# Splitting each block of weights with one operation of 1024 columns per engine, up to five steps ahead of its use

## The chip, the core and the metric

The kernel runs on one core of one Trainium2 chip. The core has a matrix engine (PE, TensorE; its weight loads are listed apart as PEld), a vector engine (DVE, VectorE), a scalar engine (ACT, ScalarE), a general engine (POOL, GpSimd) and a queue engine that here only issues transfers (SP, SyncE). Each engine works through its own instructions in the order in which they stand in its queue. An instruction that must wait for another engine holds up all that stands behind it on its own engine.

The metric is the time of one execution on the device, in microseconds (us); lower is better. A profile is a record of one execution: which instruction ran when on which engine, and what ended the idle time before it.

## The reference

The reference is a trunk of two layers over 256 tokens of width 2048. Each layer normalises its input, multiplies it by one wide matrix, gives the columns to two groups of heads and multiplies their gated outputs by a second matrix. Cut to what matters:

```python
for l in range(DEPTH):                                  # 2 layers
    h = rms_norm(x, norm_g[l])
    proj = jnp.einsum('btd,dc->btc', h, w_in[l])        # 2048 -> all heads' inputs
    rw_in, g_rw, q, k_at, v_at, g_at = jnp.split(proj, col_splits, axis=-1)
    rw_in = bidir_token_shift(rw_in, shift_mu[l])
    r, k, v, xw, xa = jnp.split(rw_in, rw_splits, axis=-1)
    y_rw = rwkv7_branch(r, k, v, xw, xa, ...)           # recurrent heads, both directions
    y_at = window_attention(rope(q), rope(k_at), v_at, sink[l])   # |i-j| <= 128
    mix = jnp.concatenate([y_rw * silu(g_rw), y_at * silu(g_at)], axis=-1)
    x = x + jnp.einsum('btc,cd->btd', mix, w_out[l])
return rms_norm(x, final_g)
```

Everything is float32. All that the change touches is how the two large products get their weights.

## The kernel before

**The large products.** A weight matrix is cut into blocks of 128x1024 numbers (512 KB); there are 280 of them in the two layers. A product of float32 numbers is made of three products in a faster number format (fp32r): the activations are kept as a rounded part and a rest (`XH`, `XL`, or `MH`, `ML` ahead of the second matrix), and each block of weights is split in the same way into `hi` (ACT copies the raw block into the rounded format, L215) and `lo` (DVE subtracts `hi` from the raw block, L216). A block serves eight **steps**, and each step is three matmuls: `XH` with `hi` (L273), `XL` with `hi` (L274), `XH` with `lo` (L275). Two blocks, or 16 steps, add up one output tile `pm` of 128x256. (Eight of the 280 blocks serve the values of the attention; they have a step of another shape, L513 to L515.) `wsplit` makes the split in two halves of 512 columns: ACT, DVE, ACT, DVE, so that the first four steps need the first half alone.

**Buffers.** `raw` has three buffers (pool `wrp`), `hi` and `lo` two each (pool `wsp`). So the split of one block cannot start before the last matmul of the block two before it has read its buffer.

**The order.** The steps of all blocks stand in one list (class `Stream`). `S.run(n)` writes down the next n steps. When the present block has `PREFETCH` steps left or fewer, it first writes down the load and the split of the next block. The function `window` writes 64 steps, in 14 slots, between which it writes the pieces of the recurrent heads (`scan_p`, `scan_i`, `scan_b`) and of the attention (`scores`, `flip`, `values`). PE runs in exactly that order. For ACT, DVE and SP a scheduler sets the order when the program is built: of the instructions that it reckons ready it takes the one that was written down first, with some pieces put ahead (`scan_b` with an offset of 95). So where a split is written down, and how long it is, changes what stands before and behind it on ACT and DVE.

**Names that the prediction uses.** One window of 64 steps uses eight blocks. In it `scan_i` of one pair of heads makes two products `pg` (L718), each masked by DVE into `ge` (L724). After the second `ge`, ACT copies out `AB` (L733), a state `suv` of `scan_b` (L890), a part of `ge` (L771), the transposed `bt` (L754) and four parts `suv` (L759), which read the PSUM tile `pt`. PE then goes on with `pq` (L803). Tiles `pg`, `pn`, `pu`, `pt`, `pyt`, `pq` and `pd` take turns in two PSUM buffers (pool `ps_w`), so PE writes one of them only when the last but one has been read out. `t` (L924) is an ACT operation at the end of `scan_b`, which reads `pyt`. `duh` (L441) is an ACT operation that waits for a transfer of `dup`. In a step of the inverse inside `scan_i`, PE's `pq` (L813) waits for DVE's predicated copies `tv` and `tt` (L822, L823).

Of the kernel before, what the change touches and what calls it, by code (L numbers as in the profile page):

```python
# [50 lines left out]
    [0, 2, 5, 7, 8, 10, 12, 13],  # L51
]
PRIO_B = 95
PREFETCH = 2


def _layout():
# [71 lines left out]
def hybrid_trunk_kernel(ctx, tc, xT, wi, wv, wo, par, fing, dup, iup, sink, pos, cst, out):  # L129
# [75 lines left out]
    def wload(src):  # L205
        raw = wrp.tile([128, 1024], F32, tag="raw", name="raw")
        SY.dma_start(out=raw, in_=src)
        return raw

    def wsplit(raw):  # L210
        hi = wsp.tile([128, 1024], F32R, tag="hi", name="hi")
        lo = wsp.tile([128, 1024], F32R, tag="lo", name="lo")
        for i in range(2):
            q = slice(i * 512, (i + 1) * 512)
            A.activation(hi[:, q], raw[:, q], AF.Copy)  # L215
            V.tensor_tensor(lo[:, q], raw[:, q], hi[:, q].bitcast(F32), op=ALU.subtract)  # L216
        return hi, lo

    def halves(src, first=None):
        return [lambda: wsplit(first if first is not None else wload(src[0])), lambda: wsplit(wload(src[1]))]  # L220

    class Stream:

# [13 lines left out]
        def run(self, n):  # L237
            for _ in range(n):
                load, steps, done = self.q[0]
                if not self.ready:  # L240
                    self.ready.append(load())
                if len(self.ready) == 1 and len(steps) <= PREFETCH and len(self.q) > 1:
                    self.ready.append(self.q[1][0]())
# [15 lines left out]
    def gemm(src, operands, evac, first=None, begin=None):  # L259

        box = []

        def step(kk):
            def f(w):
                if not box:
                    box.append(ps_main.tile([128, T], F32, tag="m", name="pm"))
                    if begin:
                        begin()
                pm = box[0]
                rh, rl = operands()  # L270
                k = kk % 8
                wh, wl = w[0][:, k * 128 : (k + 1) * 128], w[1][:, k * 128 : (k + 1) * 128]
                PE.matmul(pm, wh, rh[:, kk, :], start=(kk == 0), stop=False)  # L273
                PE.matmul(pm, wh, rl[:, kk, :], start=False, stop=False)  # L274
                PE.matmul(pm, wl, rh[:, kk, :], start=False, stop=(kk == 15))  # L275

            return f

        ld = halves(src, first)
        S.add(ld[0], [step(k) for k in range(8)])  # L280
        S.add(ld[1], [step(k) for k in range(8, 16)], lambda: evac(box[0]))
# [105 lines left out]
    def queue_inputs(l):  # L387
# [136 lines left out]
        for qt in range(4):  # L524
            S.add(
                lambda qt=qt: wsplit(wload(wv[l, qt])),
                [v_step(qt * 4 + k, b) for k in range(4) for b in range(2)],
                v_evac if qt == 3 else None,
            )
# [615 lines left out]
```

## Time and profile before

| | us |
|---|---|
| median of 3 runs (1242.3 to 1247.03) | 1244.04 |
| the profiled execution, whole | 1247.3 |
| its span, first to last instruction | 1245.5 |
| busy: PE | 1184.3 (95%) |
| busy: DVE | 937.5 (75%) |
| busy: ACT | 739.9 (59%) |
| DMA queue q1, share of 16 engines | 38.5% |

The page of the profile is an overview; matmuls overlap on PE and their ends are modelled, so its 95% says that PE is seldom seen idle, not that it runs at its best. The view of the waits sums the idle time of an engine by what ended it. The timeline lists instructions with start, length, and in brackets the idle time of the engine before them and what ended it. A view by stretches of time gives busy time and the granted clock of PE in each.

The program has three kinds of stretch: the start of a layer (about 0 to 85 us and 620 to 695 us), where the products run with little beside them; the windows with recurrent heads and attention (to about 535 us, and to about 1150 us); and the second matrix's product (the rest), where PE runs steps alone.

### The profile page before, as it was taken

The page shows a single profiled execution, that of the slowest core. Times are in us where ns is not written, and L with a number is a line of the kernel's source. Part 1 is how long each engine was busy: PE and PEld are TensorE (multiplying, and loading weights), DVE is VectorE, ACT ScalarE, POOL GpSimd, SP SyncE. Part 2 cuts the span into 40 slices and gives each one's busy share as a digit, 9 for nine tenths or more (in the row PEclk, how much of TensorE's full clock was granted, in tenths as well). Part 3 has the DMA queues.
Part 4 walks back from the last instruction along what each step waited for, and adds up shares of the span by engine and source line. Part 5 has one row for each costly group of instructions (what it writes and reads, how often), then busy time and mean ns, then how long its engine had stood idle before and what let it go on. Part 6 is the DMA issues. An engine that isn't in the chain of part 4 may idle for free.

```text
span 1245.5 us, 38032 instructions
## 1 busy us (share of the span) xinstructions
PE 1184.3 (95%) x16140; PEld 1092.3 (88%) x16140; DVE 937.5 (75%) x2082; ACT 739.9 (59%) x1838; POOL 19.0 (2%) x23
## 2 busy tenths in 40 slices
PE   6989999999998999999999999999999989999996
PEld 6978888888887989989998888888888888899996
DVE  6878878887976678856666888878887766786654
ACT  6646665766565466645555656665766555675553
POOL 0000000000000000000000000000000000000000
PEclk9999999999999999999999999999999999999998
DMA  7443233322322434466554433233223324435653
GB/s 246 156 143 122 88 116 109 105 93 94 134 77 93 133 109 142 140 204 224 210 182 143 143 110 119 93 111 109 104 93 100 112 99 131 140 130 174 212 190 119
DMA packets 60410, 166.70 MB, mean 134 GB/s; under 512 B 7728, under 2 KB 22736, under 8 KB 60240
## 3 DMA queue, kind: packets, MB, share of 16 engines
q1 hardware_dynamic: 60240, 164.27, 38.5%
q8 instruction: 126, 2.06, 0.7%
q14 instruction: 44, 0.36, 0.1%
HBM read 157.43 MB, written 4.19 MB: 130 GB/s over the span
## 4 chain that ended last, share of the span: by engine, by line
PE 48%; DVE 18%; issue 16%; ACT 11%; DMA 4%; SPq 1%; POOL 0%; DVEq 0%; POOLq 0%; ACTq 0%
PE pm L273 13%; PE pm L275 11%; PE pm L274 11%; DVE lo L216 3%; DMA g<-dup 3%; PE pg L718 2%; DVE kd L665 2%; ACT hi L215 2%; DVE ge L724 2%; ACT AB L733 2%; ACT suv L759 2%; DVE lw L659 2%; ACT ge L771 1%; DMA rrot<-u 1%; ACT bt L754 1%
## 5 line engine op out<-in xcount | busy, mean ns | idle before, releaser
L273 PE MATMUL pm<-XH,hi 128*128 128x256 f32 x1664 | 498.1, 299 | 14.5 <-ACT XH L178 6.1
L275 PE MATMUL pm<-XH,lo 128*128 128x256 f32 x1664 | 471.4, 283 | 11.2 <-DVE lo L216 11.2
L274 PE MATMUL pm<-XL,hi 128*128 128x256 f32 x1664 | 470.6, 283 | 0.1
L215 ACT ACTIVATE hi<-raw 128x512 fp32r<-128x512 f32 x560 | 329.6, 625 | 212.1 <-PE pm L274 170.0
L216 DVE TENSOR_TENSOR lo<-raw,hi 128x512 fp32r<-128x512 f32 x560 | 369.0, 687 | 84.0 <-ACT hi L215 76.7
L273 PEld LDWEIGHTS pm<-XH,hi 128*128 128x128 f32 x1664 | 316.5, 190 | 40.2 <-issue 13.0
L275 PEld LDWEIGHTS pm<-XH,lo 128*128 128x128 f32 x1664 | 316.8, 190 | 14.6 <-DVE lo L216 14.4
L274 PEld LDWEIGHTS pm<-XL,hi 128*128 128x128 f32 x1664 | 317.3, 191 | 0.8 <-DVE XL L179 0.8
L273 PE MATMUL pm<-MH,hi 128*128 128x256 f32 x512 | 145.5, 284 | 2.3 <-ACT hi L215 2.3
L275 PE MATMUL pm<-MH,lo 128*128 128x256 f32 x512 | 145.2, 284 | 0.1
L274 PE MATMUL pm<-ML,hi 128*128 128x256 f32 x512 | 145.0, 283 | 0.0
L273 PEld LDWEIGHTS pm<-MH,hi 128*128 128x128 f32 x512 | 97.9, 191 | 3.2 <-ACT hi L215 2.5
L275 PEld LDWEIGHTS pm<-MH,lo 128*128 128x128 f32 x512 | 97.8, 191 | 0.4 <-DVE lo L216 0.4
L274 PEld LDWEIGHTS pm<-ML,hi 128*128 128x128 f32 x512 | 98.0, 191 | 0.0
L890 ACT ACTIVATE suv<-pu 64x128 f32<-64x128 f32 x128 | 34.5, 270 | 24.8 <-PE pcc L888 13.6
L724 DVE TENSOR_TENSOR ge<-pg,C 128x1024 f32<-128x1024 f32 x32 | 39.1, 1221 | 3.5 <-PE pg L718 3.5
L970 ACT ACTIVATE mv<-mv,mx 128x257 f32<-128x257 f32 x64 | 31.9, 504 | 15.9 <-DVE mx L967 15.9
L733 ACT ACTIVATE AB<-ge 64x512 f16<-64x512 f32 x32 | 20.2, 630 | 34.3 <-DVE ge L724 33.9
L718 PE MATMUL pg<-mv,bk 64*128 64x128 f32 x512 | 37.2, 285 | 0.0
L822 DVE CAST_PREDICATED tv<-LV,pd 128x256 f16<-128x256 uint8 x80 | 34.0, 426 | 4.1 <-PE pd L821 3.7
L815 ACT ACTIVATE QF<-pq 128x256 f16<-128x256 f32 x80 | 30.8, 385 | 6.8 <-PE pq L813 5.5
L823 DVE CAST_PREDICATED tt<-LV,pd 128x256 f16<-128x256 uint8 x80 | 34.0, 425 | 0.0
(241 smaller groups left out, 1833.7 us busy)
## 6 DMA issues: line engine op xcount, KB each, us to landing
raw<-wi SPq DMA_DIRECT2D x207, 512.0 KB, 3.8
raw<-wo SPq DMA_DIRECT2D x64, 512.0 KB, 3.8
raw<-wv SPq DMA_DIRECT2D x8, 512.0 KB, 3.6
rrot<-u SPq DMA_DIRECT2D x80, 32.0 KB, 2.3
vg<-xT SPq DMA_DIRECT2D x16, 128.0 KB, 3.6
xd<-vg SPq DMA_DIRECT2D x16, 128.0 KB, 3.6
vg<-xd SPq DMA_DIRECT2D x16, 128.0 KB, 3.5
g<-dup SPq DMA_DIRECT2D x16, 97.0 KB
```

The costliest lines, as they stand in the source:

```text
L215: A.activation(hi[:, q], raw[:, q], AF.Copy)
L216: V.tensor_tensor(lo[:, q], raw[:, q], hi[:, q].bitcast(F32), op=ALU.subtract)
L273: PE.matmul(pm, wh, rh[:, kk, :], start=(kk == 0), stop=False)
L274: PE.matmul(pm, wh, rl[:, kk, :], start=False, stop=False)
L275: PE.matmul(pm, wl, rh[:, kk, :], start=False, stop=(kk == 15))
L718: PE.matmul(pg[:, h, c * 128 : (c + 1) * 128], BK[half[h], d, c, 1 - h : 3 - h, :].rearrange("p s j -> p (s j)"), MV[half[h], d, c].rearra ...
L724: V.tensor_tensor(GEd(d), pg.rearrange("p h (c x) -> p h c x", c=NC), gm[d].unsqueeze(1).unsqueeze(1).to_broadcast([128, 2, NC, 128]), op= ...
L733: A.activation(flat(AB[half[h]]), GE[h][half[h]].rearrange("p d c s j -> p (d c) s j")[:, :, 0, :], AF.Copy)
L822: V.copy_predicated(t_sub(TC), t_mask, flat4(pd[:, :, 0:128]))
L823: V.copy_predicated(v_sub(TT), v_mask, flat4(pd[:, 0, 128:384].rearrange("p (d x) -> p d x", d=2)))
L890: A.activation(here(h), pu[half[h], :, 0:64], AF.Copy)
L970: A.activation(Sc[:, h, q, 0:257], Sc[:, h, q, 0:257], AF.Exp, scale=0.125, bias=mx[:, q : q + 1], accum_out=den[:, q : q + 1])
```

## The change

`PREFETCH` goes from 2 to 5, so the split of the next block (and its load) is written down when five steps of the present block are left. `wsplit` makes `hi` of all 1024 columns with one ACT operation and `lo` with one DVE operation. Only the very first block, which is loaded in two halves, keeps the two halves.

```diff
-PREFETCH = 2
+PREFETCH = 5
...
-    def wsplit(raw):
+    def wsplit(raw, parts=1):
         hi = wsp.tile([128, 1024], F32R, tag="hi", name="hi")
         lo = wsp.tile([128, 1024], F32R, tag="lo", name="lo")
-        for i in range(2):
-            q = slice(i * 512, (i + 1) * 512)
+        for i in range(parts):
+            q = slice(i * 1024 // parts, (i + 1) * 1024 // parts)
             A.activation(hi[:, q], raw[:, q], AF.Copy)
             V.tensor_tensor(lo[:, q], raw[:, q], hi[:, q].bitcast(F32), op=ALU.subtract)
         return hi, lo
 
     def halves(src, first=None):
-        return [lambda: wsplit(first if first is not None else wload(src[0])), lambda: wsplit(wload(src[1]))]
+        return [lambda: wsplit(first, 2) if first is not None else wsplit(wload(src[0])), lambda: wsplit(wload(src[1]))]
```

The order of PE's instructions is the same in both programs. That of POOL is the same. On SP one load of a block in each layer moves ahead of one group of four `rrot` transfers (L494) in the attention part; all other transfers stand in the same order. ACT and DVE change in many places. Three of them follow.

The first place is ACT's queue in a window with all parts of the recurrent heads, from `AB` (L733) on. Before:

```order
L733 ACTIVATE AB<-ge 64x512 x2
L890 ACTIVATE suv<-pu 64x2x64 x2
L771 ACTIVATE ge<-mv 64x6x64
L215 ACTIVATE hi<-raw 128x512
L754 ACTIVATE bt<-pt 128x768
L759 ACTIVATE suv<-pt 64x4x64 x4
L771 ACTIVATE ge<-mv 64x6x64
```

The same place in the changed kernel:

```order
L733 ACTIVATE AB<-ge 64x512 x2
L890 ACTIVATE suv<-pu 64x2x64 x2
L771 ACTIVATE ge<-mv 64x6x64
L215 ACTIVATE hi<-raw 128x1024
L754 ACTIVATE bt<-pt 128x768
L759 ACTIVATE suv<-pt 64x4x64 x3
L924 ACTIVATE t_3615<-pyt,PR 128x256
L759 ACTIVATE suv<-pt 64x4x64
```

The split ahead of `bt` is now the whole block, and `t` (L924) has moved from behind the last `suv` to ahead of it. This order with L924 stands in 12 of the 16 windows that have a `pt`.

The second place is DVE's queue ahead of the two `ge` (L724) of the same kind of window. Before:

```order
L410 TENSOR_TENSOR g<-pm,rb 128x256
L216 TENSOR_TENSOR lo<-raw,hi 128x512 x2
L412 SCALAR_TENSOR_TENSOR vg<-g 128x256
L784 COPY tv<-EYE 128x512
L724 TENSOR_TENSOR ge<-pg,C 128x2x512
```

In the changed kernel:

```order
L410 TENSOR_TENSOR g<-pm,rb 128x256
L216 TENSOR_TENSOR lo<-raw,hi 128x1024
L412 SCALAR_TENSOR_TENSOR vg<-g 128x256
L784 COPY tv<-EYE 128x512
L724 TENSOR_TENSOR ge<-pg,C 128x2x512
```

Nothing has moved here; one operation stands where two stood, and it can start only when the whole `hi` is there.

The third place is DVE's queue in the attention, behind the softmax of one head pair (L971, L973). Before:

```order
L973 TENSOR_SCALAR mv<-mv,den 128x256 x2
L897 TENSOR_TENSOR suv<-pcc,pc 64x2x64 x2
L216 TENSOR_TENSOR lo<-raw,hi 128x512 x5
L897 TENSOR_TENSOR suv<-pcc,pc 64x2x64 x2
```

In the changed kernel:

```order
L973 TENSOR_SCALAR mv<-mv,den 128x256
L897 TENSOR_TENSOR suv<-pcc,pc 64x2x64 x2
L973 TENSOR_SCALAR mv<-mv,den 128x256
L216 TENSOR_TENSOR lo<-raw,hi 128x1024 x2
L897 TENSOR_TENSOR suv<-pcc,pc 64x2x64 x2
```

The whole `lo` of the next block stands behind the same work as its first half did before.

## The prediction, made before the changed kernel was run

> **What bounds the kernel now.** I read the page's busy times first, then a table of stretches, then the waits, then the timeline at the places where the orders differ.
>
> ```profile
> PE 1184.3 (95%) x16140; PEld 1092.3 (88%) x16140; DVE 937.5 (75%) x2082; ACT 739.9 (59%) x1838; POOL 19.0 (2%) x23
> 564.00:622.00 58.00, 58.00 (x491) 58.00 (x490) 37.45 (x70) 30.74 (x62) 0.00 (x0) 1.00 0.62 218
> 70.40:83.50 13.10, 9.86 (x75) 9.17 (x76) 13.10 (x26) 8.23 (x19) 0.00 (x0) 1.00 0.35 118
> ```
>
> The columns of the last two rows are the stretch, its length, then busy time of PE, PEld, DVE, ACT, POOL, PE's clock and DMA. In the second matrix's product (564 to 622 us) PE is never idle: 58.00 of 58.00, at full clock. A better split gives nothing there. At the start of a layer (70 to 83 us) DVE is busy 13.10 of 13.10 us and PE is not. The waits say how much PE loses to splits in all:
>
> ```profile
> ACT hi L215 <- PE pm L274: 170.0, 138, 3.5
> PE pm L275 <- DVE lo L216: 11.2, 15, 1.6
> PE pm L273 <- ACT hi L215: 6.2, 4, 2.3
> PE pq L803 <- ACT suv L759: 11.6, 12, 1.5
> PEld L813 <- DVE tt L823: 4.2, 10, 0.5
> ```
>
> (Total, times, longest.) PE waits 11.2 + 6.2 = 17.4 us for splits: the most that earlier splits can give directly. ACT, for its part, waits 170 us, in 138 cases, for PE to release a `hi` buffer. So the splits already stand at the first moment at which their buffer is free; to write them down three steps sooner cannot start those sooner. It only changes their rank against other work. The fourth row is the wait that decides the rest: in 12 windows PE waits for the last `suv`.
>
> **The change part by part.** First the price of one long operation. The trace has operations of 1024 columns on both engines (`mv`, L1042 and L1043):
>
> ```profile
> L215 ACT ACTIVATE hi<-raw 128x512 fp32r<-128x512 f32 x560 | 329.6, 625 | 212.1 <-PE pm L274 170.0 <-issue 30.5 <-PE pva L515 2.6
> L216 DVE TENSOR_TENSOR lo<-raw,hi 128x512 fp32r<-128x512 f32 x560 | 369.0, 687 | 84.0 <-ACT hi L215 76.7
> L1042 ACT ACTIVATE mv<-X 128x1024 f32<-128x1024 f32 x3 | 3.0, 1048 | 0.0
> L1043 DVE TENSOR_TENSOR mv<-mv 128x1024 f32<-128x1024 f32 x3 | 3.7, 1222 | 0.0
> 209.67 1.15 ACT L215 ACTIVATE hi<-raw 128x512 fp32r<-128x512 f32 x2 [2.73 <-PE pm L274]
> ```
>
> A half takes 625 ns on ACT and 687 on DVE, a whole 1048 and 1222. But two halves back to back take 1.15 us on ACT (last row), and 1.28 or 1.29 on DVE (below), since they overlap. So a pair saves 0.10 us of ACT and 0.07 of DVE, over 279 blocks 28 and 20 us of engine time, and none of it is PE's. Against that the first half of `hi` was there after 0.63 us, the whole is after 1.05; `lo` follows 0.42 later than its first half could.
>
> [...]
>
> *Windows with all parts (10).* ACT's queue from `AB` on, in one of them, and PE's wait:
>
> ```profile
> 173.00 1.28 ACT L733 ACTIVATE AB<-ge 64x512 f16<-64x512 f32 x2 [2.10 <-DVE ge L724]
> 174.31 0.56 ACT L890 ACTIVATE suv<-pu 64x128 f32<-64x128 f32 x2
> 174.89 0.53 ACT L771 ACTIVATE ge<-mv 64x384 f32<-64x384 f32 x1
> 175.32 0.62 ACT L215 ACTIVATE hi<-raw 128x512 fp32r<-128x512 f32 x1
> 175.97 0.81 ACT L754 ACTIVATE bt<-pt 128x768 f32<-128x768 f32 x1
> 176.79 1.55 ACT L759 ACTIVATE suv<-pt 64x256 f32<-64x256 f32 x4
> 178.91 0.57 ACT L924 ACTIVATE t<-pyt,PR 128x256 f32<-128x256 f32 x1
> 178.39 0.33 PE L803 MATMUL pq<-tv,AB 64*64 64x32 f16 x11 [0.86 <-ACT suv L759]
> ```
>
> From 173.00 to 178.34 ACT has no pause, and PE starts `pq` 0.05 us after the last `suv`, having waited 0.86. Whatever is put into this queue ahead of the last `suv` is added to PE's wait. The changed order puts in two things: the whole `hi` for a half, 1.05 - 0.62 = 0.43 us, and `t` (L924), which takes 0.57 us and so pushes the next one by about 0.47 (its neighbours overlap by 0.1). Nothing covers them: **+0.90 per window**.
>
> The second place is `ge`:
>
> ```profile
> 210.33 1.29 DVE L216 TENSOR_TENSOR lo<-raw,hi 128x512 fp32r<-128x512 f32 x2
> 211.54 0.42 DVE L412 SCALAR_TENSOR_TENSOR vg<-g 128x256 f32<-128x256 f32 x1
> 212.08 1.22 DVE L724 TENSOR_TENSOR ge<-pg,C 128x1024 f32<-128x1024 f32 x1
> 213.40 1.16 PE L718 MATMUL pg<-mv,bk 64*128 64x128 f32 x16
> 214.60 1.23 DVE L724 TENSOR_TENSOR ge<-pg,C 128x1024 f32<-128x1024 f32 x1 [0.22 <-PE pg L718]
> ```
>
> `hi` starts at 209.67, when PE releases its buffer, and the first half of `lo` at 210.33. A whole `hi` ends at 210.72, `lo` runs from 210.78 to 212.00, 0.38 later than 211.62; the first `ge` ends at 213.68 instead of 213.30. The second `pg` uses its PSUM buffer and cannot start at 213.40, but at 213.74: **+0.35**. Bounds are 0 (if PE arrives later for another reason) and 0.43. In return a late PE no longer waits for `tt` ahead of L813 (4.2 us in 10 cases, 0.42 each); DVE's own queue is mostly full up to there and moves back with it, so of 0 to 0.42 I take **-0.2**. Sum 1.05 per window, bounds 0.45 to 1.3; ten windows **+10.5** (4.5 to 13).
>
> *Last two windows with a `pt` (one per layer).* They have L924 ahead too. PE waited 1.54 for `suv` there: **+0.9 each, 1.8**.
>
> *Attention.* `lo` at the third place, twice per layer:
>
> ```profile
> 446.25 1.90 DVE L216 TENSOR_TENSOR lo<-raw,hi 128x512 fp32r<-128x512 f32 x3
> 447.11 0.28 PE L275 MATMUL pm<-XH,lo 128*128 128x256 f32 x1
> 464.37 1.89 DVE L216 TENSOR_TENSOR lo<-raw,hi 128x512 fp32r<-128x512 f32 x3
> 465.11 0.39 PE L275 MATMUL pm<-XH,lo 128*128 128x256 f32 x1 [0.99 <-DVE lo L216]
> ```
>
> DVE's work ahead is the same, so the whole `lo` ends at 447.47 and 465.59, and PE starts 0.41 and 0.53 later than it did: **+1.9** for both layers (0 to 4, as the exponentials may shift).
>
> *Block behind `duh`.* At 555 ACT stands behind a transfer in both orders, and the whole block comes after it:
>
> ```profile
> 554.73 1.13 ACT L215 ACTIVATE hi<-raw 128x512 fp32r<-128x512 f32 x2
> 555.53 1.28 DVE L216 TENSOR_TENSOR lo<-raw,hi 128x512 fp32r<-128x512 f32 x2
> 556.27 0.58 PE L275 MATMUL pm<-MH,lo 128*128 128x256 f32 x1
> ```
>
> `lo` now runs 555.84 to 557.06: PE 0.8 late, but at half clock (below), so worth 0.4 to 0.8: **+0.6**.
>
> *Starts of layers.* Here lie most of the 17.4 us, and DVE has no pause. It gains 0.07 per block, five blocks 0.35; the second halves come earlier, the first parts later, and what PE no longer waits for in the middle of a block it waits for at its head. I take **0**; the bounds are -3 (0.35 saved at each of four starts, and twice that where a wait at the head of a block goes with it) and +2 (0.42 lost at the head of one block in each). The loads stand in the same order on SP but for one per layer; a late `rrot` costs at most the 1 to 2 us until a raw buffer is free, in a stretch where PE has other steps: 0.
>
> Sum: 10.5 + 1.8 + 1.9 + 0.6 + 0 = +14.8. The profiled execution took 1247.3 (its span 1245.5), 3.3 over the median of 1244.04. So 1262 on its scale, and **1259** on the median's. The bounds together give +5 to +20: 1249 to 1264.
>
> **The rivals.** *Half clock in every window (slower still).* After two long waits close together PE ran at half clock:
>
> ```profile
> 394.80:398.10 3.30, 1.76 (x48) 1.60 (x44) 1.27 (x3) 3.20 (x7) 0.00 (x0) 1.00 0.02 5
> 398.20:401.50 3.30, 3.30 (x37) 2.96 (x35) 3.14 (x8) 2.42 (x7) 0.00 (x0) 0.50 0.03 10
> 176.30:179.60 3.30, 2.44 (x58) 2.28 (x58) 1.03 (x4) 3.20 (x8) 0.00 (x0) 1.00 0.05 12
> 1005.50:1008.80 3.30, 2.37 (x35) 2.18 (x34) 1.22 (x4) 3.10 (x8) 0.00 (x0) 1.00 0.00 0
> ```
>
> With 1.76 us busy of 3.30 the next stretch had clock 0.50; with 2.37 it had not. In a window PE is busy 2.44 of 3.30 around `pq`; 0.9 less makes 1.54. So the clock may halve ten times, each for 3.4 us, which costs up to 1.7: 5 to 17 on top, 1264 to 1276. Against it: the wait must fall into one such stretch, and steps stand close on both sides. [...]
>
> *Nothing moves on balance.* If PE's later arrival frees it from DVE's waits fully (0.42 per window), the second `pg` doesn't wait, and layer starts gain their 3, what is left is 10 x 0.48 - 3 + 1 = +3 against the median of 1244: 1247. It is also the case where the change doesn't do what it says, as ACT's 170 us of waiting suggest for the five steps.
>
> *Faster.* All 17.4 us of waits for splits vanish and ACT's queue ahead of `suv` costs nothing: 1227. For it only the waits themselves; against it the full DVE in 70.40:83.50 and ACT's unbroken 173.00 to 178.34.
>
> **How the numbers follow.** Forecast 1249 to 1264: 0.65. Half clock: 0.15. Nothing on balance: 0.14. Faster: 0.06. The range reaches from 1247 into the half-clock case, 1274. A measurement of this kernel can tell about 0.5% (6.2 us) from no change: same is 1237.8 to 1250.3, the case of nothing plus the lowest corner of the forecast, 0.16; slower 0.78, faster 0.06.
>
> **What would show it.** Right: PE's wait for `suv` (L759) at L803 rises from 0.86 to about 1.75 in ten windows, 11.6 to some 22 in sum; the distance between the same `ge` of two neighbouring windows grows by about 1; the stretch of the second matrix's product stays as long as it is; ACT's busy time at L215 falls from 329.6 to about 292 (279 x 1.048) and DVE's at L216 from 369.0 to 341 (279 x 1.222). Wrong: if that wait stays at 0.86, or if it rises and a like amount goes from L813 and L275; if the first `ge` ends as early as before; if the starts of layers lose more than 3 us of waits.

## The result, and the profile after

The changed kernel took 1265.12 us (median of 4 runs, 1262.83 to 1265.89), the kernel before 1245.53 beside it (4 runs): ratio 1.0155, interval 1.0134 to 1.0176. The forecast was 1259 in a range of 1247 to 1274, and its likeliest case, slower by a wait in each window, is what happened, though 1 us above that case's own range (1249 to 1264). Most of its terms have other sizes than I gave them.

First the page of the changed kernel: busy time of each engine, then the two groups of the split (busy time, mean ns of one, idle time before it and what ended it).

```profile
span 1263.8 us, 37504 instructions
PE 1187.7 (94%) x16140; PEld 1093.9 (87%) x16140; DVE 923.2 (73%) x1803; ACT 714.3 (57%) x1559; POOL 19.3 (2%) x23
...
L216 DVE TENSOR_TENSOR lo<-raw,hi 128x1024 fp32r<-128x1024 f32 (+1 forms) x281 | 342.4, 1219 | 130.1 <-ACT hi L215 128.4
L215 ACT ACTIVATE hi<-raw 128x1024 fp32r<-128x1024 f32 (+1 forms) x281 | 296.3, 1055 | 225.3 <-PE pm L274 186.8
```

The split itself is as cheap as it was priced: 296.3 us on ACT (forecast 292) and 342.4 on DVE (341). Both engines are less busy, and the kernel is slower. On DVE the rows of the two kernels give 369.0 - 342.4 = 26.6 us less, and none of it reached the end. Now the waits (total, times, longest):

```profile
ACT hi L215 <- PE pm L274: 186.8, 139, 4.0
DVE lo L216 <- ACT hi L215: 128.4, 172, 2.5
PE pq L803 <- ACT t L924: 15.8, 12, 2.0
PE pm L273 <- ACT hi L215: 10.0, 4, 3.5
PE pm L275 <- DVE lo L216: 9.4, 12, 1.7
PE pq L813 <- DVE tt L823: 3.9, 10, 0.6
PE pq L813 <- DVE tv L822: 3.6, 13, 0.7
PE pg L718 <- DVE ge L724: 2.8, 12, 0.2
```

Two rows of the kernel before, for PE's waits at L813:

```profile
PE pq L813 <- DVE tv L822: 1.5, 5, 0.4
PE pq L813 <- DVE tt L823: 0.9, 4, 0.3
```

ACT waits for PE to release `hi` in 139 cases against 138: five steps ahead did not start the splits sooner. The third row of the first list is the window's wait, and its releaser is new: `t` (L924) where it was `suv` (L759). Its last row did not exist before. One window, ACT and then PE:

```profile
173.45 0.53 ACT L771 ACTIVATE ge<-mv 64x384 f32<-64x384 f32 x1
173.88 1.04 ACT L215 ACTIVATE hi<-raw 128x1024 fp32r<-128x1024 f32 x1
174.95 0.81 ACT L754 ACTIVATE bt<-pt 128x768 f32<-128x768 f32 x1
175.77 1.15 ACT L759 ACTIVATE suv<-pt 64x256 f32<-64x256 f32 x3
176.83 0.55 ACT L924 ACTIVATE t<-pyt,PR 128x256 f32<-128x256 f32 x1
177.40 0.38 ACT L759 ACTIVATE suv<-pt 64x256 f32<-64x256 f32 x1
...
177.43 0.33 PE L803 MATMUL pq<-tv,AB 64*64 64x32 f16 x11 [1.34 <-ACT t L924]
...
193.38 0.30 PE L813 MATMUL pq<-tv,AB 64*64 64x32 f16 x16 [0.34 <-DVE tt L823]
...
213.12 1.16 PE L718 MATMUL pg<-mv,bk 64*128 64x128 f32 x16 [0.24 <-DVE ge L724]
```

`pq` starts at 177.43, 0.05 after `t` ends (176.83 + 0.55) and well before the last `suv` ends (177.78). So PE no longer waits for the last `suv` at all: `t` stands in its place in PE's wait, not on top of it. The wait is 1.34, against 0.86. From the start of `AB` to `pq` it is 5.87 us, against 5.39, in all twelve windows.

Where the time went is read best by stretches. The table gives the time from one block's first matmul on PE to another's (a block is 24 matmuls of L273 to L275 or their like; the core has 280, worked out from the traces, one profiled execution each). The stretches 32 to 72 and 176 to 216 hold five windows each.

| blocks | before | after | halves ahead of `bt` | halves in attention | halves at three places | half buffers, only `suv` ahead |
|---|---|---|---|---|---|---|
| start to 32 | 147.9 | 146.3 | 146.6 | 145.5 | 146.3 | 143.6 |
| 32 to 72, windows | 216.4 | 223.1 | 217.9 | 223.1 | 216.6 | 215.5 |
| 72 to 80 | 45.7 | 45.8 | 43.7 | 45.3 | 44.2 | 46.3 |
| 80 to 112, attention | 134.4 | 137.2 | 138.2 | 134.5 | 134.1 | 132.3 |
| 112 to 120, `duh` | 28.5 | 29.0 | 28.5 | 29.8 | 29.8 | 25.2 |
| 120 to 152, second matrix | 92.1 | 92.1 | 91.5 | 91.5 | 92.1 | 92.1 |
| 152 to 176, start | 113.5 | 113.6 | 112.4 | 113.5 | 113.5 | 110.5 |
| 176 to 216, windows | 215.8 | 221.8 | 218.0 | 221.6 | 216.7 | 215.1 |
| 216 to 224 | 42.2 | 44.0 | 44.8 | 44.9 | 42.7 | 42.3 |
| 224 to 248, attention | 104.1 | 106.0 | 106.1 | 104.6 | 104.6 | 102.1 |
| span | 1245.5 | 1263.8 | 1252.7 | 1259.2 | 1245.5 | 1229.8 |

Of 18.3 us the ten windows have 6.7 + 6.0 = 12.7, attention 2.8 + 1.9 = 4.7, and the second matrix nothing. In both profiled executions PE stood at half clock for about as long, 31.6 and 32.0 us in all, but not at the same places: from 72 to 80 it did so only before (3.4 us), from 216 to 224 and in the first five windows only after (3.4 us each), and behind `duh` for 6.8 us before and 3.4 after. At half clock (0.50 granted in these stretches) at most half of the time is lost, so stretches with such a difference are uncertain by up to 1.7 us.

### The profile page after: what moved, and what is told of

Its sections match the earlier page's. It is cut to its first block, busy times and chain, and to the rows that moved or that the text cites. A ratio compares the mean times of both kernels' runs of the same rounds, so it can differ in the third digit from the quotient of the medians.

```text
span 1263.8 us, 37504 instructions
## 1 busy us (share of the span) xinstructions
PE 1187.7 (94%) x16140; PEld 1093.9 (87%) x16140; DVE 923.2 (73%) x1803; ACT 714.3 (57%) x1559; POOL 19.3 (2%) x23
## 5 line engine op out<-in xcount | busy, mean ns | idle before, releaser
L273 PE MATMUL pm<-XH,hi 128*128 128x256 f32 x1664 | 499.1, 300 | 15.1 <-ACT hi L215 6.6
L275 PE MATMUL pm<-XH,lo 128*128 128x256 f32 x1664 | 473.0, 284 | 9.0 <-DVE lo L216 8.7
L216 DVE TENSOR_TENSOR lo<-raw,hi 128x1024 fp32r<-128x1024 f32 (+1 forms) x281 | 342.4, 1219 | 130.1 <-ACT hi L215 128.4
L215 ACT ACTIVATE hi<-raw 128x1024 fp32r<-128x1024 f32 (+1 forms) x281 | 296.3, 1055 | 225.3 <-PE pm L274 186.8
L273 PEld LDWEIGHTS pm<-XH,hi 128*128 128x128 f32 x1664 | 317.4, 191 | 41.3 <-issue 13.0
L275 PEld LDWEIGHTS pm<-XH,lo 128*128 128x128 f32 x1664 | 318.0, 191 | 12.9 <-DVE lo L216 12.7
L273 PE MATMUL pm<-MH,hi 128*128 128x256 f32 x512 | 144.8, 283 | 3.5 <-ACT hi L215 3.5
L275 PE MATMUL pm<-MH,lo 128*128 128x256 f32 x512 | 144.6, 283 | 0.8 <-DVE lo L216 0.8
L273 PEld LDWEIGHTS pm<-MH,hi 128*128 128x128 f32 x512 | 97.4, 190 | 4.4 <-ACT hi L215 3.7
L275 PEld LDWEIGHTS pm<-MH,lo 128*128 128x128 f32 x512 | 97.3, 190 | 1.0 <-DVE lo L216 1.0
L890 ACT ACTIVATE suv<-pu 64x128 f32<-64x128 f32 x128 | 34.2, 267 | 20.7 <-PE pq L813 10.4
L724 DVE TENSOR_TENSOR ge<-pg,C 128x1024 f32<-128x1024 f32 x32 | 39.0, 1220 | 4.4 <-PE pg L718 4.1
L733 ACT ACTIVATE AB<-ge 64x512 f16<-64x512 f32 x32 | 20.1, 629 | 38.6 <-DVE ge L724 38.2
L718 PEld LDWEIGHTS pg<-mv,bk 64*128 64x128 f32 x512 | 31.1, 187 | 6.0 <-DVE ge L724 4.4
```

Source lines behind the costliest of these rows:

```text
L718: PE.matmul(pg[:, h, c * 128 : (c + 1) * 128], BK[half[h], d, c, 1 - h : 3 - h, :].rearrange("p s j -> p (s j)"), MV[half[h], d, c].rearra ...
L724: V.tensor_tensor(GEd(d), pg.rearrange("p h (c x) -> p h c x", c=NC), gm[d].unsqueeze(1).unsqueeze(1).to_broadcast([128, 2, NC, 128]), op= ...
L733: A.activation(flat(AB[half[h]]), GE[h][half[h]].rearrange("p d c s j -> p (d c) s j")[:, :, 0, :], AF.Copy)
L890: A.activation(here(h), pu[half[h], :, 0:64], AF.Copy)
```

## The experiments

**Which half of the change costs?** Theory A: the one long operation. Rival B: the five steps, which change the rank of `lo` on DVE. Each half of the change alone:

```diff
 the changed kernel, two steps:
-PREFETCH = 5
+PREFETCH = 2
 the kernel before, five steps:
-PREFETCH = 2
+PREFETCH = 5
```

> The change's kernel with splits two steps ahead as before: the one operation alone. Theory A (the single long operation costs; the five steps change only rank): the loss of 1.0155 stays, 1.013 to 1.020 of before, 1262 to 1270 us, with PE's wait at L803 again behind the last suv or t at some 1.3 us per window. Rival B (the five steps cost, since lo goes ahead of DVE's tv and tt): the time returns to before, 1.000 to 1.004, and L813's waits for tt and tv return from 6.3 + 3.9 + 3.6 to 4.2 + 0.9 + 1.5 us.

> The kernel before with splits five steps ahead, halves kept: the five steps alone. Theory A: no change, 0.997 to 1.003, as ACT waits for PE to release hi in some 140 cases either way; L803's wait stays near 0.86 per window. Rival B: most of the loss, 1.009 to 1.016, with L813's waits for tt and tv up as in the change's kernel.

Measured: one operation with two steps 1266.59 us, ratio to before 1.0179 (1.0159 to 1.0200); halves with five steps 1244.82, 0.9992 (0.9977 to 1.0007). B falls; the five steps alone change nothing that can be measured, and ACT waits for PE's release of `hi` in 133 cases there. With the one operation alone, the waits have the change's form:

```profile
PE pq L803 <- ACT t L924: 17.3, 12, 2.0
PE pq L813 <- DVE tt L823: 3.8, 10, 0.6
PE pg L718 <- DVE ge L724: 2.9, 12, 0.2
```

**Where does it cost?** The changed kernel, with halves again at chosen blocks. For the twelve ahead of `bt`:

```diff
+    nsplit = iter(range(1000))
     def wsplit(raw, parts=1):
+        if next(nsplit) % 140 in (38, 46, 54, 62, 70, 78):
+            parts = 2
```

Ahead of the first `ge` the list is (45, 53, 61, 69, 77), in the attention `range(80, 112)`, and the fourth kernel has all three.

> The change's kernel, but the twelve blocks whose hi stands ahead of bt in ACT's queue (six per layer) are split in halves. Theory A with this place: L803's wait falls from 1.34 back to 0.86 per window, 12 x 0.48 = 5.8 us, 0.994 to 0.997 of the change's kernel (1257 to 1261). Rival C (the wait at L803 only stands in for another one just behind it): L803's wait falls but L813's rises by a like amount, under 2 us in all. The half-clock stretch at 310 us may go too, 1.5 us.

> The change's kernel, but the ten blocks whose lo stands ahead of the first ge of a window in DVE's queue are split in halves. Theory A with this place: the second pg's wait for ge (2.8 + 4.4 us on PE and its loads, 0.24 each in ten windows) goes, 2 to 3 us of the loss, 0.997 to 0.9985 of the change's kernel (1261 to 1263). Rival C: the time is taken up by L803 or L813 behind it, under 0.5 us.

> The change's kernel with halves in 32 blocks around the attention of each layer (blocks 80 to 111 of 140) and whole blocks elsewhere. Theory A (the whole lo there is late by some 0.4 to 0.7 us at the blocks for which DVE's queue is full): the 4.6 us that these stretches lost come back, 0.9955 to 0.9975 of the change's kernel, 1259 to 1261. Rival (the loss came with the other order behind the last window, not with the length): under 1 us.

> The change's kernel with halves ahead of bt, ahead of the first ge, and around the attention, and whole blocks at the 95 or so other places of a layer. Theory A (the loss sits at these three places and the whole operation is free elsewhere): 10.5 + 1.5 + 4.5 us come back, 1247 to 1250, 0.999 to 1.004 of the kernel before. Rival (the whole operation costs a little everywhere, through ACT and DVE): 1253 or more, 1.006 and up.

| halves | median us | to before (interval) | span |
|---|---|---|---|
| ahead of `bt` | 1254.53 | 1.0085 (1.0068 to 1.0102) | 1252.7 |
| ahead of the first `ge` | 1263.91 | 1.0156 (1.0139 to 1.0173) | 1261.9 |
| in the attention | 1260.25 | 1.0123 (1.0109 to 1.0137) | 1259.2 |
| at all three | 1244.98 | 0.9995 (0.9984 to 1.0007) | 1245.5 |

Ahead of `bt`, more came back than expected: 11.1 us of span, not 5.8. Its waits at L803 and L813:

```profile
PE pq L803 <- ACT suv L759: 11.5, 12, 1.6
PE pq L813 <- DVE tv L822: 3.8, 9, 0.9
PE pq L813 <- DVE tt L823: 1.4, 3, 0.6
PE pg L718 <- DVE ge L724: 2.8, 12, 0.2
PE pza L622 <- DVE tt L809: 3.3, 10, 0.6
```

The order ahead of the last `suv` is the old one, and the wait at L803 with it (11.6 before). Of the 11.1 us, 9.0 lie in the ten windows. There L803 gives back 4.9 and L813 3.4, but a wait for `tt` at L622 (last row), which the changed kernel does not have, takes 3.3 again. So rival C, that one wait stands in for another, holds for L813 and L622, but not for L803. One stretch at half clock is gone as well (up to 1.7), and the rest is in no wait that the profile lists. Halves ahead of `ge` leave PE 0.9 of its 2.8 us of waits for `ge`. In the trace the distance between the same `ge` of two neighbouring windows falls from 44.0 to 43.7 us (42.9 before the change). That is too little for the comparison of times, which shows no difference from the change (1.0156 against 1.0155). Halves in the attention give 4.6 us of span back, 4.1 of it there (134.5 and 104.6 in the table). With all three the span is that of before, though 193 of 280 blocks are still split whole. So on balance the whole operation is free at those, and the loss sits at these three places; for the place ahead of `ge` the times alone do not show it.

**Is it ACT's length alone?** `hi` in halves at the twelve blocks ahead of `bt`, `lo` whole everywhere:

```diff
             A.activation(hi[:, q], raw[:, q], AF.Copy)
-            V.tensor_tensor(lo[:, q], raw[:, q], hi[:, q].bitcast(F32), op=ALU.subtract)
+        V.tensor_tensor(lo, raw, hi.bitcast(F32), op=ALU.subtract)
```

> The change's kernel with hi alone in halves at the twelve blocks ahead of bt, lo whole. If ACT's length ahead of bt is the cause there (theory A): as with both in halves, 1254 to 1257, L803's wait behind suv at 0.9 to 1.0. If DVE's length matters as well (the whole lo holds up tt): L803's wait comes back, L813's stays at 6.3 + 3.9 us, 1258 to 1261.

1285.57 us, 1.0325 of before (1.0308 to 1.0343): neither. PE's two waits in one window, and what ACT and DVE did ahead of the second:

```profile
176.74 0.33 PE L803 MATMUL pq<-tv,AB 64*64 64x32 f16 x11 [0.83 <-ACT suv L759]
180.26 0.39 PE L275 MATMUL pm<-XH,lo 128*128 128x256 f32 x1 [1.57 <-DVE lo L216]
...
177.26 0.56 ACT L924 ACTIVATE t<-pyt,PR 128x256 f32<-128x256 f32 x1
177.73 0.62 ACT L215 ACTIVATE hi<-raw 128x512 fp32r<-128x512 f32 x1
...
178.99 1.22 DVE L216 TENSOR_TENSOR lo<-raw,hi 128x1024 fp32r<-128x1024 f32 x1
```

L803's wait is as before the change, though `lo` is whole: it was set by ACT's queue (the length of `hi`, and the place of `t`, which came back with the halves), not by DVE. But the second half of `hi` now stands behind `t` on ACT, and a whole `lo` needs both: it starts at 178.99 and PE waits 1.57 for it, and after several of these waits the clock halved (last section; the mean granted clock was 0.977, against 0.987 in the changed kernel's profiled execution). Halves paid here only where both engines had them (1254.53 against 1285.57), so that the first half went all the way to PE.

**What if nothing stands ahead of `suv`?** In the kernel before, `hi` of the twelve blocks was queued behind the last `suv` (a no-wait edge in the order, `issue_after`); then also the two copies into `ge` (L771). In the changed kernel the whole `hi` was queued so:

```diff
+            if n in (38, 46, 54, 62, 70, 78):
+                es.enter_context(tc.issue_after(suv_read[-1]))
             ...
             for h in range(2):
+                with tc.issue_after(suv_read[-1]):
                     A.activation(c3(GE[h]...), c3(MV...), AF.Copy)
```

> The kernel before (halves, two steps), with the hi of the twelve blocks ahead of bt queued on ACT behind the last suv of its step. Theory A (what stands ahead of the last suv in ACT's queue is added to PE's wait): L803's wait falls from 0.86 to some 0.3 per window, 12 x 0.55 = 6.6 us less if nothing else is late, 1239 to 1243, 0.995 to 0.998 of before. Rival (the block of weights is then late, or L813 and tt bound at once behind it): within 0.2% of before.

> The kernel before with both fillers of ACT's queue, the hi of the twelve blocks and the two copies into ge (L771 there), queued behind the last suv of their step, so that bt and suv follow AB and the other suv at once. Theory A (the queue ahead of the last suv is PE's wait, 0.53 us of ge and 0.62 of hi): L803's wait of 0.86 goes to 0 in ten windows and from 1.54 to some 0.4 in the last two, 8 to 11 us less, 1234 to 1238, 0.992 to 0.995 of before. Rival (hi or ge are then late in turn, and PE waits at L275 or L866 instead): within 0.3% of before.

> The change's kernel, its whole hi of the twelve blocks queued behind the last suv. Theory A: L803's wait falls from 1.34 to 0.85, as a ge takes the place ahead; but the block's first use is some 1 us behind the last suv, and a whole hi and a whole lo need 1.05 + 1.2 us from there, so PE waits for lo at L275 by some 1.5 us in each window instead: 1270 to 1280, 1.02 to 1.03 of before. Rival (place alone counts, not length): as with halves ahead of bt, 1252 to 1256.

`hi` alone behind `suv`: 1243.67, 0.9992 (0.9981 to 1.0003), a miss. The scheduler filled the place with the second `ge`, and L803's wait stayed 0.85. With `ge` behind too: 1247.66, 1.0013 (1.0003 to 1.0024). The wait at L803 fell from 11.6 us to 0.5 in one case, and two others stand in one window in its stead:

```profile
178.42 0.39 PE L273 MATMUL pm<-XH,hi 128*128 128x256 f32 x1 [0.49 <-ACT hi L215]
179.26 0.39 PE L275 MATMUL pm<-XH,lo 128*128 128x256 f32 x1 [0.33 <-DVE lo L216]
```

0.49 + 0.33 = 0.82 for 0.86: the rival, nearly one for one. The whole `hi` behind `suv` took 1261.55, 1.0126 (1.0109 to 1.0142), less bad than expected, and worse than its rival: L803 0.85, and PE waits 0.40 for `lo`, not 1.5, since `lo` starts on DVE at once when `hi` is done (177.82). In a window ACT has one half of `hi` to place ahead and one behind, and the kernel before does just that.

**Sooner buffers.** If PE's release of `hi` is what a split waits for, tiles of half a block free it sooner, in the same memory. First alone (halves, five steps), then with the second half of `hi` and the `ge` copies behind `suv`:

```diff
-        hi = wsp.tile([128, 1024], F32R, tag="hi", name="hi")
-        lo = wsp.tile([128, 1024], F32R, tag="lo", name="lo")
+        hi = [wsp.tile([128, 512], F32R, tag=f"hi{i}", name="hi") for i in range(2)]
+        lo = [wsp.tile([128, 512], F32R, tag=f"lo{i}", name="lo") for i in range(2)]
```

> Halves five steps ahead, and hi and lo each in two tiles of 512 columns (the same memory), so that PE releases the first half's buffer half a block (1.4 us) sooner. Theory A: PE's waits for hi and lo (6.2 + 11.2 us in the kernel before) fall by up to half, but in the windows the second half of hi now stands ahead of bt where the first stood, so L803's wait stays at 0.86: 1236 to 1243, 0.992 to 0.998 of before. Rival (DVE is full where those waits lie, so sooner buffers bring nothing): 0.998 to 1.002.

> As the half buffers, and the second half of hi of the twelve blocks and the two copies into ge queued behind the last suv. Theory A: with the first half of hi split before AB, moving the rest behind the last suv no longer makes PE wait for the block: L803's wait goes (0.86 in ten windows, some 1.2 in two) and none comes at L273 or L275 for it, 8 to 11 us less than the half buffers alone, 1226 to 1235, 0.984 to 0.992 of before. Rival (lo or tt is late in turn, as DVE is): within 0.3% of the half buffers alone.

Alone: 1246.66, 0.9991 (0.9974 to 1.0008), a miss, and the rival's number. Together: 1232.31, **0.988** (0.9862 to 0.9897), faster than both kernels. The waits, of the half buffers alone and of both:

```profile
PE pq L803 <- ACT suv L759: 11.0, 11, 1.0
PE pq L813 <- DVE tt L823: 10.4, 10, 1.1
PE pm L275 <- DVE lo L216: 5.3, 8, 2.0
```

```profile
PE pza L622 <- DVE tt L809: 7.6, 10, 0.8
PE pm L275 <- DVE lo L216: 5.7, 8, 2.0
PE pq L813 <- DVE tt L823: 3.8, 10, 1.1
```

The total came out in the expected range, though 14.4 us below the half buffers alone and not 8 to 11; the reason did not come out as expected. The wait at L803 is gone (0.5 us is left, in one case), but a wait of 0.8 for `tt` (L809) takes its place ahead of L622, and the windows are nearly as long as before (215.5 and 215.1 for five, against 216.4 and 215.8). The gain over before lies at the layer starts, 4.3 + 3.0, behind `duh`, 3.3, and in the attention, 2.1 + 2.0. Waits for splits account for a part of it: those for `lo` at L275 fell from 11.2 us to 5.7, those for `hi` at L273 from 6.2 to 5.1. The clock may account for another part, in these two executions: the one of before stood at half clock for 6.8 us behind `duh` and 3.4 at the second start, this one at neither (up to 3.4 and 1.7 us). The ratio 0.988 is not the clock, as its mean over all runs is 0.990 here and between 0.989 and 0.990 before; where the gain lies is shown in part only. The half buffers alone win some 7 us at these places, but their windows are 3.8 + 4.7 us longer, with PE waiting for `tt` at L813 (10.4 us); the second kernel takes that back. Which of the two edits behind `suv` it needs was not tried.

## Why the prediction was right, and where not

The sum said +14.8; the spans differ by 18.3. The windows cost 12.7 and not 10.5, the attention 4.7 and not 1.9, the starts gave 1.5 back, and the second matrix's product stayed at 92.1 us.

- **What bounds.** Right. Splits already start when PE releases their buffer: five steps alone, 0.9992.
- **L803 in ten windows, +0.90.** Too large: 1.34 - 0.86 = 0.48. The step that failed is the one that `t` "pushes the next one by about 0.47". PE's wait ended with `t`, before the last `suv`. Why `pq` no longer needs that `suv`, I read from the order and did not test: `pq` takes one of two PSUM buffers, and its releaser says that it now takes the one that `t` reads. The other part, 0.43 for the long `hi`, was right by the rows: from the start of the `hi` to that of `bt` 0.65 us before, 1.07 after; from the first `suv` to `pq` 1.60 and 1.66. No run changes the one without the other, as halves bring back both the old length and the old order.
- **Second `pg`, +0.35.** Too large: 0.24.
- **L813, -0.2.** Wrong sign, from a misread row: the 0.42 per window is a wait of the weight loads (PEld). PE itself waited there for 0.6 us in the ten windows, so a late PE could win 0.06 in each and no more. PE's rows of L813 grew by 5.1 us over the run (3.9 + 3.6 against 0.9 + 1.5), 3.8 of it in the ten windows, 0.4 each. I took DVE's queue to move with PE; halves ahead of `bt` took most of this wait away, but put one at L622 in its place.
- **The windows' sum, 1.05.** 0.48 + 0.24 + 0.4 = 1.1: right by luck, as one term was too large and another had the wrong sign. The stretches give 1.2 to 1.35 per window, with one stretch at half clock in the first layer.
- **Last two windows, 1.8.** 0.1 and 1.8 in their stretches (72 to 80, 216 to 224): 1.9 in sum, by luck. PE's wait at L803 went from 1.54 to 2.03 in the first and to 0.55 in the second, not up by 0.9 in each, and each difference holds 3.4 us of half clock, in the first before the change, in the second after. With halves ahead of `ge` alone the wait is 2.0 in both; why it was 0.55 here stays open.
- **Attention, +1.9.** Mis-sized: 2.8 + 1.9 = 4.7, over my bound of 4. I counted two places per layer, by what `lo` alone would lose. In the first layer there were four waits for `lo` (2.4 us against 1.0 in one case), and waits for `tv` at L813 and L829 grew by 0.8, which I had not looked at. In the second layer there were two for `lo` (1.9 us against 1.0 in one case).
- **Block behind `duh`, +0.6.** 0.5, by luck. PE waited 0.8 for `lo` as I had it, but also 1.2 longer for the whole `hi` (3.5 us at L273 against 2.3), which I had left out; 3.4 us less at half clock hid up to 1.7 of it.
- **Starts, 0.** -1.6 at the first, 0.1 at the second: within the bounds. At the first, waits for `lo` fell from 5.5 to 1.9 us and those for `hi` at the head of a block rose from 2.5 to 4.5, as I had it.
- **Half clock in every window.** Did not happen: one of ten in the profiled execution. It did in six of ten in the kernel with `lo` whole and `hi` in halves, below. Some of the 19.6 us between the medians may still be half clock: the mean granted clock of the changed kernel's four runs was 0.986, that of 17 runs of the kernel before, beside the first experiments, 0.990. As an estimate from these, that is some 10 us more at half clock, worth up to 5.

## What to carry to other kernels

A long instruction on an in-order engine that another engine waits for costs where it stands, not what it saves (here DVE was busy 26.6 us less at L216, and the span grew by 18.3): look for the places where its first half is wanted at once, or where a short and urgent copy is queued behind it, and split it there alone; 193 whole blocks of 280 cost nothing here on balance. Ahead of time in the program is not sooner if the buffer isn't free (five steps alone: 0.9992): smaller buffers, in the same memory, halved PE's waits for `lo` (11.2 to 5.3 us), though the kernel was faster only with ACT's queue put in order as well. And a wait that is taken away is not yet a gain: in these windows 0.86 us moved from L803 to L273 and L275 (0.82), or to L622 (0.8).

## What had not been expected of the hardware

Half clock after a wait that is far shorter than the stretch. The kernel with `hi` in halves and `lo` whole, stretches around its waits of 1.57 or 1.58 us in two neighbouring windows, and two more (PE, PEld, DVE, ACT and POOL busy, then PE's clock and DMA):

```profile
178.45:181.85 3.40, 1.82 (x32) 1.40 (x32) 3.40 (x7) 2.47 (x6) 0.00 (x0) 1.00 0.16 36
181.85:185.25 3.40, 3.40 (x18) 3.40 (x17) 2.25 (x6) 1.80 (x6) 0.00 (x0) 0.50 0.76 261
222.80:226.21 3.41, 1.94 (x29) 1.68 (x28) 2.04 (x4) 3.36 (x7) 0.00 (x0) 1.00 0.00 0
226.21:229.62 3.41, 3.08 (x43) 2.85 (x44) 3.12 (x8) 1.80 (x6) 0.00 (x0) 1.00 0.50 154
314.96:318.37 3.41, 1.83 (x14) 1.62 (x15) 2.73 (x6) 2.75 (x6) 0.00 (x0) 1.00 0.00 0
318.37:321.78 3.41, 3.41 (x49) 3.18 (x47) 3.12 (x7) 2.42 (x7) 0.00 (x0) 1.00 0.65 193
```

The half-clock periods of this trace start on one grid: 181.8, 274.0, 362.8, 407.1 and 574.4 us lie 27, 26, 13 and 49 steps of 3.41 us apart. Those of each of the other 13 traces lie on such a grid too. The first wait (178.69 to 180.26) falls into one step of the grid: PE was busy 1.82 of 3.40 us, and the clock was 0.50 in the next. The second (224.96 to 226.54) falls across two steps, with 1.94 and 3.08 busy, and the clock stayed 1.00. So the same wait can cost the clock or not by where it falls. That alone does not decide: after the step at 314.96, with 1.83 busy, the clock stayed 1.00.

Counted over the steps at full clock in all 14 traces, without the first 15 us and all behind 1215 us: of 34 steps with PE busy for less than 1.6 us, 33 were followed by half clock; from 1.6 to 2.0 us it was 23 of 70, from 2.0 to 2.6 us 5 of 232, above that none of 4492. So a price for half clock must be a chance and not a sum. What decides between 1.6 and 2.0 us stays open.
